# Column order of the input projection in a two-layer hybrid encoder: both gates of HGRN heads 0 and 1 first, the queries second, and the HGRN work beside the third unit

## The chip, the cores and the metric

The kernel runs on one core of one Trainium2 chip. The metric is the device time of one execution in microseconds (us). An execution of the kernel before took 1639.49 us in the median of 3 runs (1636.96 to 1640.6). Engines are named as in the profile: PE (TensorE matmuls), PEld (its weight loads), DVE (VectorE), ACT (ScalarE), POOL (GpSimd), SP (SyncE, which issues the weight loads from memory here).

## What is computed

One sequence of 512 tokens with 1024 features goes through two layers. Each layer has a mixer and then a mixture of 16 experts. The mixer projects the normalised input with one matrix of 4608 columns, and cuts the result into nine groups of 512 columns:

```
proj = xn @ w_in                      # (512, 1024) x (1024, 4608)
rq, rk, rv, rg, hq, hf_fwd, hf_bwd, hi, hg = split(proj, 9)
q = rotary(rq); k = rotary(rk) * 128**-0.5          # 4 retention heads
r_out = rms(retention(q, k, rv)) * ret_g * silu(rg)
q2 = silu(hq) * 128**-0.5;  v2 = hi                 # 4 HGRN heads of 128
f  = lb + (1 - lb) * sigmoid(z);  k = (1 - lb) * sigmoid(-z)   # z = hf_fwd or hf_bwd
h_out = rms(hgrn(q2, k_f, v2, log f_f) + reversed hgrn with f_b, k_b) * hgrn_g * silu(hg)
h = x + concat(r_out, h_out) @ w_out
```

Each HGRN head needs its query, its forward gate and its backward gate; the values v2 are needed only by the last part of its recurrence. The first layer has lb = 0.

## The kernel before, in words

**The projection.** `plan` queues the weight loads in the order of `GROUPS`: column group 4 (hq), 5 (hf_fwd), 6 (hf_bwd), 7 (hi), 0, 1, 2, 3 (the retention groups) and 8 (hg). I call the nine projections unit 0 to unit 8, in the order in which they run. A unit has 96 matmuls of 128x512 and takes four PSUM banks, one for each 128 columns (c = 0 to 3). Its weights come in two loads of 1 MB (512 rows by 512 columns). `split` (L423) cuts them into four parts of 256 rows. ACT rounds a part to the matmul's format (L436, "copy"), and DVE subtracts the rounded part from the part (L438, "low part"); for the odd parts of the units with columns 7 and 2 POOL does the subtraction. Every product is a sum of three matmuls, two with the rounded part and one with the low part. Unit n is cut into quarters q = 0 to 3, one for each part; at the start of quarter q the code issues the split of the next part, 4n+q+1. The four banks are complete one after the other in the last quarter, and each is evacuated there: `silu_q` (one ACT, one DVE instruction), `forget` (two ACT instructions, in the second layer two of DVE as well), `copy_out` (one ACT), `rotate` (two ACT of 64 partitions, one DVE, one POOL, and one DVE addition that `add_late` issues with the next bank).

**The work beside it.** `proj` yields after every six matmuls, 16 times in a unit. I call these steps 1 to 16. After each step `lead` (L812) adds a budget to a credit that begins at 0 in each unit, and while the credit is above 0 it issues the next piece of the work beside the projection and takes off the piece's cost. Nothing here is measured at run time: budgets (`BUDGET`, L420) and costs are constants, and each engine runs its instructions in the order of issue. So the pieces' places are worked out by adding.

**The HGRN pieces** (`hgrn_pair`, heads 0 and 1, then heads 2 and 3), each once per head, with its cost:

- A (1.2): POOL adds the two keys (L568), DVE multiplies gates and queries (L569).
- B (1.2): two DVE products (L579, L580), ACT rounds them (L582), POOL subtracts (L583).
- C (1.3): two DVE products (L551, L556), two ACT copies that make the keys of the next level (L531), one POOL product (L561).
- D (0.65): four PE products with `parity` (L591), one DVE product (L594).
- L1 to L6 (1.9 each, the two heads by turns): four PE products with the keys that the piece of this head before it made (L604), the same two DVE products, two ACT copies and one POOL product as C, and one DVE selection (L606).
- T (0.4): transposes (L619) and ACT copies; S (1.0): products (L644) and DVE sums (L650), the first that read v2; O (0.5): outputs (L663).

In the kernel before the pieces of heads 0 and 1 begin beside unit 3 with budget 1.0 (A, A, B, B, C in steps 1 to 5, C in 7, D in 8 and 9). Those of heads 2 and 3 begin at the last step of unit 4 (budget 1.2) and go on beside unit 5 (budget 1.0: B, B in steps 2 and 3, C, C in 4 and 5, D, D in 7, level pieces in 8, 10, 12, 14, 16) and unit 6 (budget 0.9: level pieces in steps 1, 3, 5 and so on). Unit 7 (budget 2.2) has the rest of them, then `retention`, whose pieces are keys (1.0), outputs (0.6) and states (1.0) by head, and then four splits of the output weights (L806 ACT, L807 two on POOL and two on DVE). The keys of head 0 come in step 1 and its states in step 2. The last outputs and two output splits come in step 6, the other two splits in step 7.

Of the kernel before, what the change touches and what calls it, by code (L numbers as in the profile page):

```python
# [16 lines left out]
P = 128  # L17
S = 512
# [47 lines left out]
class Kernel:  # L66
# [55 lines left out]
    def plan(self):  # L122
        a = self.a
        for l in range(self.depth):
            for g in self.GROUPS:
                for j in range(2):
                    n = 2 if g == self.GROUPS[0] and j == 0 else 1
                    self.wq.append((("in", l, g, j),
                                    [a["w_in"][l, j * 512 + i * (512 // n):j * 512 + (i + 1) * (512 // n),
                                               g * 512:(g + 1) * 512]  # L130
                                     .rearrange("(k p) c -> p k c", p=P) for i in range(n)], [n, 4 // n, 512]))
            for f in range(2):
                for j in range(2):
                    self.wq.append((("out", l, f, j), a["w_out"][l, j * 512:(j + 1) * 512, f * 512:(f + 1) * 512]
                                    .rearrange("(k p) c -> p k c", p=P), [4, 512]))
            for q in range(NE // 2):

                for j in range(2 if q == 0 else 0):
                    for nm in ("w_gate", "w_up"):
                        self.wq.append(((nm, l, -1, j), [a[nm][l, e, :2 * P].rearrange("(p k) c -> k p c", k=2)[j]  # L140
                                                         for e in range(2)], [2, 1024]))
                for j in range(q == 0, 4):
                    for nm in ("w_gate", "w_up"):
                        for e in (2 * q, 2 * q + 1):
                            self.wq.append(((nm, l, e, j), a[nm][l, e, j * 256:(j + 1) * 256, :]
                                            .rearrange("(p k) c -> p (k c)", k=2), [2, 1024]))
                if q < NE // 2 - 1:
                    for j in range(4):
                        for e in (2 * q, 2 * q + 1):
                            self.wq.append((("w_down", l, e, j), a["w_down"][l, e, j * 256:(j + 1) * 256, :]  # L150
                                            .rearrange("(p k) c -> p (k c)", k=2), [2, 1024]))
                else:
                    for i, (lo, n) in enumerate(PIECES):
                        m = 1024 // n
                        for j in range(ND // m):
                            self.wq.append((("w_down", l, i, j),
                                            [a["w_down"][l, e, j * m * P:(j + 1) * m * P, lo:lo + n]
                                             .rearrange("(k p) c -> p k c", p=P) for e in (2 * q, 2 * q + 1)],
                                            [2, m, n]))
# [14 lines left out]
    def load(self, key, src, shape):  # L174
        t = self.slot(shape)
        for i, part in enumerate(src if isinstance(src, list) else [src]):
            dst = t[:, i] if isinstance(src, list) else t

            self.nc.sync.dma_start(dst if len(part.shape) > 2 or isinstance(src, list) else dst.rearrange("p k c -> p (k c)"), part)
        self.loaded[key] = t  # L180
# [236 lines left out]
    WAITS, RATE = (1, 1, 2), 0.7  # L417
    EARLY = 5
    COSTS = (1.2, 1.3, 0.65, 1.9)
    BUDGET = (1.0, 1.2, 1.0, 0.9, 2.2, 1.3)  # L420
    GROUPS = (4, 5, 6, 7, 0, 1, 2, 3, 8)

    def split(self, upto):  # L423


        nc = self.nc
        while self.nsplit <= min(upto, 4 * len(self.GROUPS) - 1):
            i = self.nsplit
            self.nsplit += 1
            g, j, jj = self.GROUPS[i // 4], i % 4 // 2, i % 2  # L430
            if jj == 0:
                self.raw = self.take(("in", self.mix_layer, g, j))
            part = self.slot([2, 2, 512], F32R)
            wh, low = part[:, 0], part[:, 1]
            src = self.raw.rearrange("p a k c -> p (a k) c")[:, 2 * jj:2 * jj + 2]
            nc.scalar.activation(wh, src, AF.Copy)  # L436
            e = nc.gpsimd if self.GROUPS[i // 4] in (7, 2) and i % 2 or i == 0 else nc.vector
            e.tensor_tensor(low, src, wh, op=OP.subtract)  # L438
            self.parts[i] = part
            if jj:  # L440
                self.put(self.raw)
# [31 lines left out]
    def forget(self, l, d, c, ps):  # L473

        nc = self.nc
        F, K = self.F[c // 2][:, c % 2, d], self.K[c // 2][:, c % 2, d]
        nc.scalar.activation(F, ps, AF.Sigmoid)
        nc.scalar.activation(K, ps, AF.Sigmoid, scale=-1.0)
        if l > 0:
            lb, om = self.lb[:, c:c + 1], self.omlb[:, c:c + 1]  # L480
            nc.vector.tensor_scalar(F, F, om, lb, op0=OP.mult, op1=OP.add)
            nc.vector.tensor_scalar(K, K, om, None, op0=OP.mult)
# [51 lines left out]
    def hgrn_pair(self, hp):  # L534
# [6 lines left out]
        Q = self.slot([2, 2, S])  # L541
        AT, T, Tn, kt, B = {}, {}, {}, {}, {}

        def ascend(c, n, m):
# [7 lines left out]
            if 2 * m < P:  # L552
                kt[c] = self.level_keys(B[c][:, n % 2], k0, 2 * m)
            qv = self.view(q0, 0, [[S + m, 2], [2 * m, J], [1, m]])
# [9 lines left out]
        for c in heads:  # L564
            hh = c % 2
            B[c] = self.slot([4, S])
            AT[c], Tn[c] = B[c][:, 2], B[c][:, 3]
            nc.gpsimd.tensor_tensor(AT[c], K[:, hh, 0], K[:, hh, 1], op=OP.add)  # L568
# [4 lines left out]
        for c in heads:  # L573


            q0, k0, x = Q[:, c % 2], K[:, c % 2], B[c][:, :2]
            X[c] = self.slot([2, 2, S], F32R)
# [32 lines left out]
        for c in heads:  # L610
            part = lambda x: x[:, :3 * P].rearrange("p (b t) -> p b t", b=3)
            W[c] = [part(B[c][:, 0]), part(B[c][:, 1]), part(F[:, c % 2, 0]), part(F[:, c % 2, 1])]
        for c in heads:
# [211 lines left out]
    def mixer(self, l):  # L825
        nc = self.nc
        self.norm1(l)
        self.rope = self.tmp4([2, S])
        nc.sync.dma_start(self.rope, self.a["rope"])
        if l == 0:  # L830
            self.const_rows()
        self.lead(self.proj(0, False, self.silu_q))
        if l == 0:
            self.more_consts()
        self.F = [self.slot([2, 2, S]) for _ in range(2)]
        self.K = [self.slot([2, 2, S]) for _ in range(2)]
        for n, d in ((1, 1), (2, 0)):
            self.lead(self.proj(n, False, lambda c, ps: self.forget(l, d, c, ps)))
        self.oh = None
        self.hsq = self.t2.tile([P, S], F32, name=f"hsq{l}", tag="tn", bufs=1)  # L840
        hg = self.hgrn()
        B = self.BUDGET
        self.lead(self.proj(3, True, lambda c, ps: self.copy_out("v2", c, ps)), hg, B[0])
        self.left = ()
        for n, nm in ((4, "rq"), (5, "rk")):
            self.lead(self.proj(n, False, lambda c, ps: self.rotate(nm, c, ps)), hg, B[n - 3])
        self.add_late()
        self.lead(self.proj(6, True, lambda c, ps: self.copy_out("rv", c, ps)), hg, B[3])
        wo = self.wout_split(l)

        def eighth():
            yield from hg
            yield from self.retention()
            for _ in range(4):
                yield next(wo)
        side = eighth()
        self.lead(self.proj(7, False, lambda c, ps: self.gate_out("rg", 4 * l, c, ps)), side, B[4])
        for _ in side:
            pass

        def ninth():
            yield from self.norms()
            yield from wo
        side = ninth()
        self.lead(self.proj(8, False, lambda c, ps: self.mix_out(8 + 4 * l, c, ps)), side, B[5])
        for _ in side:
            pass
        self.put(*self.xH, *self.xL, self.oh)
        self.load_h(self.hd if l > 0 else self.xv)
        self.xe = self.slot([ND, 2 * P])  # L870
        self.pump()
        self.output(l)
# [497 lines left out]
```

## Time and profile before

| | |
|---|---|
| median of 3 runs | 1639.49 us (1636.96 to 1640.6) |
| profiled execution | 1637.67 us, of which the span is 1635.8 us |
| granted TensorE clock, mean | 0.977 of full speed |
| PE busy | 1531.0 us (94%) |
| DVE, ACT, POOL busy | 664.4, 474.9, 229.3 us |
| units 0 to 8, layer 0 | from 15.4 to about 298 us of the span |
| units 0 to 8, layer 1 | from 821.6 to about 1107 us of the span |

The span runs from the first to the last instruction; the profiled execution took 1.87 us more than its span. A line of the timeline has start, duration, engine, source line, operation, tiles, shape and count, and in brackets how long the engine was idle before it and what ended that. Neighbouring instructions of one kind are merged. A stretch's clock is the share of the full TensorE clock that was granted.

### The profile page before, as it was taken

To read this page: it belongs to the slowest core of one execution; us is meant where nothing else is said; L and a number is where in the kernel's file an instruction comes from. 1 tells how busy PE (TensorE), PEld (TensorE's weight loads), DVE (VectorE), ACT (ScalarE), POOL (GpSimd) and SP (SyncE) were. 2 spreads that over 40 slices of the span, in tenths; PEclk is the share of its full clock that TensorE was granted. 3 is DMA by queue.
4 is the path that set the end of the run, shared out by engine and by line. 5 is a ranking of instruction groups with operands and counts; after the bars stand their busy time and mean duration, and the time that the engine had idled before them with its cause. 6 is when DMAs were issued, how large, how long until landed. Compare 5 with 4: busy or idle time off the path is not lost. (4 is left out here: it accounts for less than half of the span.)

```text
span 1635.8 us, 19932 instructions
## 1 busy us (share of the span) xinstructions
PE 1531.0 (94%) x7970; PEld 954.9 (58%) x7970; DVE 664.4 (41%) x1107; ACT 474.9 (29%) x889; POOL 229.3 (14%) x201
## 2 busy tenths in 40 slices
PE   7989899969999999999999899999699999999986
PEld 6878798754354534533478787977444445444333
DVE  5378945561121312212254889464511122212113
ACT  4334444542221200200343434455322202112003
POOL 3042542100000000011021344430000000000201
PEclk9999999989999999999999999999799999999998
DMA  7211132577999999999941211317699999999997
GB/s 262 75 53 52 52 124 78 211 303 301 427 425 426 427 426 427 426 427 427 400 176 51 78 41 64 123 52 258 273 385 427 420 427 426 427 427 426 426 426 275
DMA packets 94605, 464.53 MB, mean 284 GB/s; under 512 B 7904, under 2 KB 16288, under 8 KB 48432
## 3 DMA queue, kind: packets, MB, share of 16 engines
q1 hardware_dynamic: 93040, 458.35, 69.0%
q0 software_dynamic: 1472, 4.90, 0.8%
q8 instruction: 63, 1.03, 0.2%
q14 instruction: 30, 0.25, 0.0%
HBM read 459.03 MB, written 4.19 MB: 283 GB/s over the span
## 5 line engine op out<-in xcount | busy, mean ns | idle before, releaser
L1145 PE MATMUL pj<-s,s 128*64 128x512 f32 x2048 | 478.8, 599 | 19.2 <-DMA s<-in_w_up_dram 13.9
L465 PE MATMUL pj<-s,s 128*128 128x512 f32 x1728 | 426.7, 401 | 12.9 <-DVE s L438 8.6
L465 PEld LDWEIGHTS pj<-s,s 128*128 128x128 f32 x1728 | 324.2, 192 | 82.7 <-DVE s L438 11.6
L1145 PEld LDWEIGHTS pj<-s,s 128*64 128x64 f32 x2048 | 173.3, 137 | 279.6 <-issue 203.3
L1265 PE MATMUL pb<-s,t 128*64 128x512 f32 x896 | 197.8, 594 | 5.4 <-ACT t L1183 2.7
L1272 POOL TENSOR_TENSOR s<-s,s 128x1024 f32<-128x1024 f32 x8 | 18.7, 2362 | 872.1 <-DVE s L1205 823.5
L1265 PEld LDWEIGHTS pb<-s,t 128*64 128x64 f32 x896 | 66.0, 137 | 126.8 <-issue 110.8
L1193 DVE SCALAR_TENSOR_TENSOR t<-pb,sm,t 128x512 fp32r<-128x512 f32 (+1 forms) x34 | 24.5, 719 | 242.5 <-ACT t L1192 241.0
L1205 DVE TENSOR_TENSOR s<-s,pb 128x512 f32<-128x512 f32 (+1 forms) x112 | 67.3, 661 | 130.0 <-PE pb L1200 130.0
L909 PE MATMUL pj<-s,s 128*128 128x512 f32 x384 | 96.6, 400 | 3.4 <-DVE s L796 2.9
L438 DVE TENSOR_TENSOR s<-s,s 128x1024 fp32r<-128x1024 f32 x62 | 84.3, 1383 | 37.8 <-ACT s L436 37.6
L1110 DVE COPY sm<-pb 128x2 f32<-128x2 f32 x16 | 2.5, 159 | 210.9 <-PE pb L1107 210.9
L909 PEld LDWEIGHTS pj<-s,s 128*128 128x128 f32 x384 | 69.3, 189 | 20.7 <-DVE s L796 4.6
L1192 ACT ACTIVATE t<-pb,sm 128x512 fp32r<-128x512 f32 (+1 forms) x34 | 22.5, 662 | 195.4 <-PE pb L1265 183.2
L1088 PEld LDWEIGHTS pb<-t,t 128*128 128x128 f32 x512 | 64.9, 199 | 17.3 <-issue 15.0
L1121 ACT ACTIVATE t<-pb 128x512 fp32r<-128x512 f32 x16 | 9.6, 601 | 221.0 <-PE pb L1119 221.0
L436 ACT ACTIVATE s<-s 128x1024 fp32r<-128x1024 f32 x72 | 73.4, 1048 | 0.0
L1088 PE MATMUL pb<-t,t 128*128 128x256 f32 x512 | 69.8, 293 | 3.2 <-DVE t L1072 2.4
L1200 PE MATMUL pb<-t,t 128*128 128x512 f32 (+1 forms) x256 | 66.7, 401 | 0.1
L556 DVE TENSOR_TENSOR s<-s,s 128x512 f32<-128x512 f32 x56 | 59.3, 1059 | 13.4 <-PE pb L604 13.4
L1200 PEld LDWEIGHTS pb<-t,t 128*128 128x128 f32 x256 | 44.7, 188 | 33.0 <-issue 19.4
L531 ACT ACTIVATE s<-s 128x256 f32<-128x256 f32 x96 | 35.3, 415 | 93.8 <-DVE s L551 93.5
(237 smaller groups left out, 1541.2 us busy)
## 6 DMA issues: line engine op xcount, KB each, us to landing
s<-in_w_gate_dram SPq DMA_DIRECT2D x124, 1024.0 KB, 19.5
s<-in_w_up_dram SPq DMA_DIRECT2D x124, 1024.0 KB, 19.6
s<-in_w_down_dram SPq DMA_DIRECT2D x112, 1024.0 KB, 19.6
s<-in_w_in_dram SPq DMA_DIRECT2D x34, 1024.0 KB, 5.9
s<-in_w_down_dram SPq DMA_DIRECT2D x32, 512.0 KB, 9.4
s<-in_w_out_dram SPq DMA_DIRECT2D x8, 1024.0 KB, 4.8
s<-in_x_dram SPq DMA_DIRECT2D x8, 512.0 KB
s<-in_w_gate_dram SPq DMA_DIRECT2D x8, 512.0 KB, 5.6
```

What stands on the lines that cost most here:

```text
L436: nc.scalar.activation(wh, src, AF.Copy)
L438: e.tensor_tensor(low, src, wh, op=OP.subtract)
L465: nc.tensor.matmul(pg[c], lhsT=lhsT, rhs=rhs, start=(k == 0 and m == 0), stop=(k == ND - 1 and m == 2))
L531: self.nc.scalar.activation(kv[:, :, e], src, AF.Copy)
L556: v.tensor_tensor(qv, qv, tq, op=OP.mult)
L909: nc.tensor.matmul(po, lhsT=x, rhs=w, start=(k == 0 and i == 0), stop=(k == ND - 1 and i == 2))
L1088: nc.tensor.matmul(pt[:, i], lhsT=x[:, tt, k % 2::2], rhs=oh[:, tt], start=(tt == 0 and x is self.picked[u][0]), stop=(tt == NT - 1 and x ...
L1145: nc.tensor.matmul(pg[n + 2 * f][e * CAP:(e + 1) * CAP], lhsT=self.xe[:, k, at + e * CAP:at + (e + 1) * CAP], rhs=w[e][:, f * 512:(f + 1) ...
L1193: v.scalar_tensor_tensor(yL[0][:, cs], py, gate, yH[0][:, cs], op0=OP.mult, op1=OP.subtract)
L1200: nc.tensor.matmul(pc, lhsT=ohT[:, tt * P:(tt + 1) * P], rhs=y[:, cs], start=(y is yH[0]), stop=(y is yL[0]))
L1205: v.tensor_tensor(dst, dst, pc, op=OP.add)
L1265: nc.tensor.matmul(py[f][e * CAP:(e + 1) * CAP], lhsT=hT[:, k, e * CAP:(e + 1) * CAP], rhs=W[e][:, k2, f * 512:(f + 1) * 512], start=(k == ...
```

## The change

`GROUPS` becomes `UNITS`, a list of column starts. Unit 0 now has the first 256 columns of hf_fwd and the first 256 of hf_bwd (both gates of heads 0 and 1). Unit 1 has the queries. Unit 2 has the other halves of the two gates. Units 3 to 8 have the columns that they had. The loads of units 0 and 2 are cut by columns: twice as many DMAs, in rows of 1 KB instead of 2 KB, of 256 KB for the first half of unit 0 and of 512 KB else. The HGRN pieces begin beside unit 2, with new budgets. The POOL subtractions stay with the odd parts of units 3 and 6. No arithmetic is added or left out.

```diff
     def plan(self):
...
-            for g in self.GROUPS:
+            for g, unit in enumerate(self.UNITS):
                 for j in range(2):
-                    n = 2 if g == self.GROUPS[0] and j == 0 else 1
+                    n = 2 if g == j == 0 else 1
+                    m, w = 4 // n, 512 // len(unit)
                     self.wq.append((("in", l, g, j),
-                                    [a["w_in"][l, j * 512 + i * (512 // n):j * 512 + (i + 1) * (512 // n),
-                                               g * 512:(g + 1) * 512]
-                                     .rearrange("(k p) c -> p k c", p=P) for i in range(n)], [n, 4 // n, 512]))
+                                    [((slice(i * m, (i + 1) * m), slice(e * w, (e + 1) * w)),
+                                      a["w_in"][l, j * 512 + i * m * P:j * 512 + (i + 1) * m * P, at:at + w]
+                                      .rearrange("(k p) c -> p k c", p=P)) for i in range(n) for e, at in enumerate(unit)], [4, 512]))
...
-    BUDGET = (1.0, 1.2, 1.0, 0.9, 2.2, 1.3)
-    GROUPS = (4, 5, 6, 7, 0, 1, 2, 3, 8)
+    BUDGET = (0.95, 0.95, 0.9, 0.9, 1.4, 1.3, 0.9)
+    UNITS = ((2560, 3072), (2048,), (2816, 3328), (3584,), (0,), (512,), (1024,), (1536,), (4096,))
...
-            e = nc.gpsimd if self.GROUPS[i // 4] in (7, 2) and i % 2 or i == 0 else nc.vector
+            e = nc.gpsimd if g in (3, 6) and i % 2 or i == 0 else nc.vector
...
     def forget(self, l, d, c, ps):
+        if c // 2 not in self.F:
+            self.F[c // 2], self.K[c // 2] = self.slot([2, 2, S]), self.slot([2, 2, S])
...
-        self.lead(self.proj(0, False, self.silu_q))
+        self.F, self.K = {}, {}
+        self.lead(self.proj(0, False, lambda c, ps: self.forget(l, 1 - c // 2, c % 2, ps)))
         if l == 0:
             self.more_consts()
-        self.F = [self.slot([2, 2, S]) for _ in range(2)]
-        self.K = [self.slot([2, 2, S]) for _ in range(2)]
-        for n, d in ((1, 1), (2, 0)):
-            self.lead(self.proj(n, False, lambda c, ps: self.forget(l, d, c, ps)))
+        self.lead(self.proj(1, False, self.silu_q))
...
         hg = self.hgrn()
         B = self.BUDGET
+        self.lead(self.proj(2, False, lambda c, ps: self.forget(l, 1 - c // 2, 2 + c % 2, ps)), hg, B[-1])
         self.lead(self.proj(3, True, lambda c, ps: self.copy_out("v2", c, ps)), hg, B[0])
```

Unit 2 gets budget 0.9, unit 3 0.95, units 4 to 6 get 0.95, 0.9 and 0.9, unit 7 gets 1.4 and unit 8 keeps 1.3.

## Rows read from the trace of the kernel before

**Rows 1.** Page: busy time of engines; a group's count, busy, mean ns, idle before.

```profile
PE 1531.0 (94%) x7970; PEld 954.9 (58%) x7970; DVE 664.4 (41%) x1107; ACT 474.9 (29%) x889; POOL 229.3 (14%) x201
...
L436 ACT ACTIVATE s<-s 128x1024 fp32r<-128x1024 f32 x72 | 73.4, 1048 | 0.0
```

**Rows 2.** PE's waits, 80 to 275 us (layer 0): us in total, times, longest.

```profile
PE pb L591 <- POOL s L583: 4.5, 3, 2.2
PE pj L465 <- DVE s L438: 3.7, 2, 2.0
PE pb L604 <- ACT s L531: 2.4, 1, 2.4
```

**Rows 3.** Timeline of PE: units 1 to 3 of layer 0, then of layer 1.

```profile
54.73 39.16 PE L465 MATMUL pj<-s,s 128*128 128x512 f32 x172
...
96.55 1.01 PE L591 MATMUL pb<-s,parity 128*128 128x512 f32 x2 [2.19 <-POOL s L583]
...
99.95 2.50 PE L465 MATMUL pj<-s,s 128*128 128x512 f32 x5 [1.96 <-DVE s L438]
...
835.83 65.36 PE L465 MATMUL pj<-s,s 128*128 128x512 f32 x287 [0.99 <-DVE s L438]
...
908.64 2.50 PE L465 MATMUL pj<-s,s 128*128 128x512 f32 x5 [2.19 <-DVE s L438]
```

**Rows 4.** Timelines of DVE and POOL, start of unit 3, layer 0.

```profile
88.81 2.18 DVE L579 TENSOR_TENSOR s<-s,s 128x512 f32<-128x512 f32 x1 [6.65 <-POOL s L568]
...
96.47 3.42 DVE L438 TENSOR_TENSOR s<-s,s 128x1024 fp32r<-128x1024 f32 x1 [2.07 <-ACT s L436]
...
103.91 1.27 DVE L594 TENSOR_TENSOR s<-pb,two 128x512 f32<-128x512 f32 x2
...
93.43 5.38 POOL L583 TENSOR_TENSOR s<-s,s 128x1024 fp32r<-128x1024 f32 x2 [3.40 <-ACT s L582]
```

**Rows 5.** Timeline of PE: end of unit 4 and start of the second pair, layer 0.

```profile
144.77 1.50 PE L644 MATMUL pb<-s,s 128*128 128x128 f32 x12
...
150.22 4.63 PE L663 MATMUL pb<-s,s 128*128 128x128 f32 x40
...
165.63 1.20 PE L591 MATMUL pb<-s,parity 128*128 128x512 f32 x4 [0.75 <-POOL s L583]
168.41 1.17 PE L591 MATMUL pb<-s,parity 128*128 128x512 f32 x2 [1.58 <-POOL s L583]
```

**Rows 6.** Stretches of layer 0: length, busy by engine, granted clock, DMA share, GB/s.

```profile
169.00:173.00 4.00, 4.00 (x17) 3.32 (x16) 4.00 (x3) 0.57 (x2) 3.80 (x3) 0.64 0.55 177
196.00:201.00 5.00, 5.00 (x21) 4.16 (x20) 5.00 (x6) 0.98 (x4) 3.90 (x4) 0.68 0.00 0
```

**Rows 7.** Timelines of DVE, ACT and PE around the end of unit 5, layer 0.

```profile
182.35 1.22 DVE L438 TENSOR_TENSOR s<-s,s 128x1024 fp32r<-128x1024 f32 x1 [0.56 <-ACT s L436]
...
184.18 1.28 DVE L523 TENSOR_TENSOR s<-s,t 128x512 f32<-128x512 f32 x1
...
188.80 0.59 ACT L513 ACTIVATE t<-pj 64x512 f32<-64x512 f32 x1
...
194.40 0.72 ACT L531 ACTIVATE s<-s 128x256 f32<-128x256 f32 x2 [3.19 <-DVE s L551]
...
195.18 1.54 PE L604 MATMUL pb<-s,s 128*128 128x128 f32 x8 [2.42 <-ACT s L531]
```

**Rows 8.** Timelines of PE, ACT and DVE in unit 7 of layer 0.

```profile
231.15 1.64 PE L465 MATMUL pj<-s,s 128*128 128x512 f32 x6
...
267.17 6.87 PE L465 MATMUL pj<-s,s 128*128 128x512 f32 x29 [1.74 <-DVE s L438]
...
231.21 1.05 ACT L723 ACTIVATE s<-pb,dec_k 128x384 f32<-128x384 f32 x2 [0.51 <-PE pb L720]
...
258.00 3.90 ACT L806 ACTIVATE s<-s 128x1024 fp32r<-128x1024 f32 x4
...
260.05 5.93 DVE L807 TENSOR_TENSOR s<-s,s 128x1024 fp32r<-128x1024 f32 x2 [5.93 <-ACT s L806]
```

More of the change, by code (lines that the diff above doesn't have):

```diff
@@ L177, in load @@
             dst = t[:, i] if isinstance(src, list) else t
+            if isinstance(part, tuple):
+                (k, cols), part = part
+                dst = t[:, k, cols]
             self.nc.sync.dma_start(dst if len(part.shape) > 2 or isinstance(src, list) else dst.rearrange("p k c -> p (k c)"), part)
@@ L419 @@
     COSTS = (1.2, 1.3, 0.65, 1.9)
-    BUDGET = (1.0, 1.2, 1.0, 0.9, 2.2, 1.3)
-    GROUPS = (4, 5, 6, 7, 0, 1, 2, 3, 8)
+    BUDGET = (0.95, 0.95, 0.9, 0.9, 1.4, 1.3, 0.9)
+    UNITS = ((2560, 3072), (2048,), (2816, 3328), (3584,), (0,), (512,), (1024,), (1536,), (4096,))
     def split(self, upto):
         nc = self.nc
-        while self.nsplit <= min(upto, 4 * len(self.GROUPS) - 1):
+        while self.nsplit <= min(upto, 4 * len(self.UNITS) - 1):
             i = self.nsplit
             self.nsplit += 1
-            g, j, jj = self.GROUPS[i // 4], i % 4 // 2, i % 2
+            g, j, jj = i // 4, i % 4 // 2, i % 2
             if jj == 0:
@@ L434, in split @@
             wh, low = part[:, 0], part[:, 1]
-            src = self.raw.rearrange("p a k c -> p (a k) c")[:, 2 * jj:2 * jj + 2]
+            src = self.raw[:, 2 * jj:2 * jj + 2]
             nc.scalar.activation(wh, src, AF.Copy)
-            e = nc.gpsimd if self.GROUPS[i // 4] in (7, 2) and i % 2 or i == 0 else nc.vector
+            e = nc.gpsimd if g in (3, 6) and i % 2 or i == 0 else nc.vector
             e.tensor_tensor(low, src, wh, op=OP.subtract)
```

## The prediction

> **What bounds the kernel now.** I read the page first: PE is busy for 94% of the span [rows 1], so the change, which keeps every product, can only touch PE's waits and the clock that PE is granted. Then I read PE's waits by what ended them. In units 1 to 7 of layer 0 they come to 10.6 us [rows 2], and layer 1 repeats the pattern, with a longer part at the start of the first pair. The timeline puts them at four places: the start of the first pair of HGRN heads in unit 3 (2.19 and 1.96 us, [rows 3]), the start of the second pair in unit 5 (0.75 and 1.58, [rows 5]), the rotation at the end of unit 5 (2.42, [rows 7]) and the output splits in unit 7 (1.74, [rows 8]). The stretches come last. After the second and the third place the granted clock averages 0.64 over 4 us and 0.68 over 5 us [rows 6], so PE spent part of these stretches at the lower of its two levels (1.2 instead of 2.4 GHz); against the full clock that is 4 x 0.36 = 1.4 and 5 x 0.32 = 1.6 us lost. After the fourth it isn't so: 29 matmuls took 6.87 us [rows 8], 0.24 us each. If every one of these waits went, with the clock that they cost, the two layers would gain under 30 us. That is the most that the change could do.
>
> A step of six matmuls takes 6 x 39.16/172 = 1.37 us [rows 3], half a unit 10.93. I add the pieces' costs against the new budgets as the code does, and follow each engine's queue from the start of a unit.
>
> **The start of the first pair (now unit 2).** The pieces stand at the same steps as before (A, A, B, B in 1 to 4), so the low part of the third quarter is again issued behind B on DVE and behind its rounding on ACT. Before, unit 3 of layer 0 began 10.93 us before the end of the first row of [rows 3], at 82.96, and PE went on with the third quarter at 99.95, 17.0 us later; in layer 1 it began at 890.26 and went on at 908.64, 18.4 us later. Now POOL has no subtraction in this unit and its key sums run early, since the gates are two units old. The queries come last: bank 3 is evacuated by ACT (0.6, as the 0.59 of [rows 7]), then part 9 is rounded (1.05, [rows 1]) and subtracted (1.22, [rows 7]) until about 2.9; the two A products of the same size end at 5.3; the first B product I put at 1.1, between the half of 1.22 and the 2.18 of the row beside POOL. So it ends at 6.4. From the end of that product to the end of the low part the row has 99.89 - 90.99 = 8.9 us, since the subtraction takes 3.42 us beside POOL's pair of 5.38 us [rows 4]. The low part is there at 15.3 and PE, which wants it at 11.2, waits 4.1 us. It goes on 1.7 us earlier than before in layer 0 and 3.1 in layer 1, less the first D piece, which then fell into the wait and now doesn't (4 products, 0.9 us): **-0.8 and -2.2 us**. The bounds are none and all of the old waits (4.15, and in layer 1 the 1.4 more). The loss of clock that follows I leave as it was.
>
> **The start of the second pair (now unit 4).** T, T and S of the first pair are in step 1 of unit 4, S in 2, O in 3 and 4, A in 5 and 6, B in 7 and 8. S takes 1.3 us and T the same, O half of 4.5 [rows 5], so the first O ends at about 3 x 1.37 + 3 x 1.3 + 2.2 = 10.2. Behind its copy part 18 is rounded and subtracted until 13.1; A, A and one B product last until 16.5, and 8.9 us later, at 25.4, part 19 is ready. PE wants it after 12 steps, 8.4 us of T, S and O and 0.9 of D, at 25.7. So there is no wait, and the 2.33 us and the 1.4 us of clock go: **-3.8 us** in each layer. Bounds: -3.8 and, if the DVE comes 3 us later, 0. The three pieces in step 1 cost 0.2 us, as S waits for T's copies (0 to 0.4).
>
> **The rotation at the end of unit 4.** What is late next is here. Before, only T, S and O lay beside it, and nothing waited. Now C is in steps 10 and 11, D in 12 and 13, the level pieces in 14 and 16 and then in 1 and 3 of unit 5: the same places as those of level pieces at the end of unit 5 before, where the one of step 3 waited 2.42 us. The C pieces are over 103.91 - 90.99 = 12.9 us after the B product [rows 4], at 29.4. Behind them are part 20's rounding, then the rotation. Before, it took 6.45 us from the low part (182.35) to the end of the first key copy (188.80, [rows 7]); without the addition of an older bank (1.28) and with one D product (0.64) it takes 5.8, from 30.6 to 36.4. PE is at the piece of step 1 at 35.2: 1.2 us of wait. From ACT's start on the next bank to the end of the next key copy the rows have 195.12 - 188.80 = 6.3 us, so that is at 42.7, and PE wants it at 40.0: 2.65 us. With the clock of the row (1.6) this is **+5.4 us** in each layer. Bounds: 0, as here before, and +7.
>
> **The rotation at the end of unit 5.** The level pieces are in steps 13 and 15 and in 1 and 3 of unit 6, one step earlier than those that were late. Both keys are in time by the same queue; but ACT, which waits for DVE in its order of issue, gets to bank 3 and to POOL's part 25 later, and PE waits some 0.9 and 1.7 us for them, with a clock as after 0.75 and 1.58 (1.4). The old place cost 2.42 + 1.6. **0**; bounds -4.0 and +2.
>
> **Unit 7.** The keys of head 0 and its states now fall into one step. ACT's two copies between them end 1.05 + 0.06 us after PE is through with the keys [rows 8], which six matmuls covered before: **+1.1 us** (bounds 0 and 1.6). The output splits stand in steps 8 and 9, on both sides of part 31. From the end of the last outputs at 256.75 in the rows, PE would want part 31 after four steps, at 262.4. DVE has the first output split from 260.05 on, 2.96 us beside POOL [rows 8], then part 31 at the same pace with the cover of POOL ending before it does: 265.5. That is 3.1 us in place of 1.74: **+1.4 us**, bounds 0 and +3.7 (1.6 of it clock, if the longer wait costs any).
>
> A rule of the Trainium skill bears on this term: the page SBUF — State Buffer, section SBUF: two separate sides, says that of a DVE operation with two SBUF inputs and a GpSimd operation the one that starts first holds their shared ports for the whole instruction. The low part's 3.42 against 1.22 us agrees. By it part 31 would come either before or wholly behind POOL's second split, not in between.
>
> **At nothing.** The loads of units 0 and 2 move the same bytes in narrower rows; the copies that read the loads had ACT idle for 0.0 us in all before them [rows 1], and in layer 0 PE's first product waits for the norm. ACT's eight evacuations at the end of unit 2 lie beside key copies that PE wants two steps later; if that cover fails, it is a wait like the 1.2 us above, in layer 1 first, where DVE has eight more instructions.
>
> **Sum.** Layer 0: -0.8 - 3.8 + 0.2 + 5.4 + 0 + 1.1 + 1.4 = +3.5; layer 1: +2.1; together +5.6 us. The profiled execution took 1637.67 us, 1.8 less than the median of the runs shown, so the sum gives 1643.3 against it and 1645.1 against the median. I say 1644.
>
> **Rivals.**
> 1. *The rotation of unit 4 hides its keys* (faster). One mechanism: C and D end 4 us sooner on DVE, because POOL's long products miss them. For it: beside unit 4 POOL has no subtraction left. Against it: C's own POOL products follow at once on B's. Then 5.4 us a layer go: 5.6 - 10.8 = -5.2, 1633; if the end of unit 5 is free as well, -13, 1626. It decides at a gain of over 2 us in DVE's queue at C.
> 2. *Gains and losses meet* (no change). Only one of the two waits of unit 4 is there, or the splits of unit 7 cost nothing: 2.8 less or 2.5 less, 1641 with either.
> 3. *DVE gets the ports first in unit 7*: part 31 ends at 260.05 + 2.96 + 1.22 = 264.2, a wait of 1.8, and the term is 0: 1641. The rule of the page in the sentences above is the other way to this result.
> 4. *The gates of unit 2 fill ACT* (slower still). Key copies behind eight evacuations, then POOL's part 13 late: 1.2 us and a clock of 1.6 in each layer, 1650. The copies' lead of two steps speaks against it.
>
> **How the numbers follow.** Forecast 0.39, rivals 0.29, 0.13, 0.07 and 0.12. A difference of 0.2% (3.3 us) can be told from no change. Faster 0.29 is rival 1. Slower is rival 4 and 0.32 of the forecast's 0.39, the rest of which lies under 3.3 us: 0.44. No change: 0.27. The range goes from half-way between rival 1's two times to a little above rival 4: 1629 to 1652; the forecast's own is 1639 to 1650.
>
> **What would show it.** Right: PE's wait for L438 in unit 2 near 4 us; no wait for L583 in unit 4; two waits for L531 in the first three steps of unit 5; a wait for L723 of about 1 us at the start of unit 7; part 31 late by 3 us. Wrong: unit 5 begins without a wait, or unit 2 or 3 has waits that unit 3 did not have before.

## The result: 0.8% slower

Four runs of the changed kernel took 1650.76 to 1653.41 us, median 1651.85; four of the kernel before 1636.96 to 1640.6, median 1638.45. The ratio is 1.0081, with a 95% interval of 1.0064 to 1.0099: 13.4 us slower. The forecast was 1644, between 1629 and 1652, slower with a chance of 0.44. The sign was right, the loss two to three times the +5.6 of the sum. The time lies 0.15 us below the upper end of the range, above the forecast's own 1639 to 1650, and nearest to the 1650 of rival 4, whose waits the trace does not show. The ratios of the experiments below leave out two executions far above the rest, one of the kernel before (1683.45 us, beside numbers 5 to 7) and one of number 8 (8694.58 us), the only one of number 8 with a trace.

**The profile after.** On the page PE is busy for 5.5 us longer than in [rows 1], in a span that is 15.8 us longer; the rest is idle time. Little of the 5.5 us lies in the stretches that the change touches (0.5 us in layer 0, 0.9 in layer 1).

```profile
PE 1536.5 (93%) x7970; PEld 955.4 (58%) x7970; DVE 659.2 (40%) x1107; ACT 476.6 (29%) x889; POOL 227.6 (14%) x201
```

Where does it lie? The first product after unit 8 (L909 before, L916 after) closes the stretch that the change touches. PE's timeline has it in layer 0 and layer 1, first before, then after:

```profile
298.64 1.65 PE L909 MATMUL pj<-s,s 128*128 128x512 f32 x6 [0.26 <-DVE t L790]
...
821.56 3.75 PE L465 MATMUL pj<-s,s 128*128 128x512 f32 x14 [1.51 <-ACT s L398]
...
1107.75 4.15 PE L909 MATMUL pj<-s,s 128*128 128x512 f32 x17 [0.26 <-DVE t L790]
```

```profile
305.78 4.15 PE L916 MATMUL pj<-s,s 128*128 128x512 f32 x17 [0.20 <-DVE t L798]
...
829.69 2.61 PE L471 MATMUL pj<-s,s 128*128 128x512 f32 x9 [1.51 <-ACT s L402]
...
1121.50 2.79 PE L916 MATMUL pj<-s,s 128*128 128x512 f32 x11 [0.18 <-DVE t L798]
```

Layer 0 loses 305.78 - 298.64 = 7.1 us, and layer 1, whose first product was at 821.56 before, (1121.50 - 829.69) - (1107.75 - 821.56) = 5.6: 12.7 of the 13.4. Two layers were predicted to lose 3.5 and 2.1.

PE's waits in layer 0, by what ended them (total, times, longest), answer to [rows 2]. The wait for POOL's subtraction in the B pieces (L583 there, L591 here) is gone from the list, the wait for subtractions (L438 there, L444 here) has nearly doubled, and L612 now waits twice:

```profile
PE pj L471 <- DVE s L444: 6.6, 3, 3.3
PE pb L612 <- DVE s L564: 2.9, 1, 2.9
PE pb L612 <- ACT s L539: 1.7, 1, 1.7
```

The timeline of PE gives each its place. Behind the end of unit 1 they are, mostly in pairs, the start of the first pair in unit 2, the start of the second pair in unit 4 (one row), the rotation at the end of unit 4, that at the end of unit 5, the pieces in unit 6, and unit 7.

```profile
39.30 32.93 PE L471 MATMUL pj<-s,s 128*128 128x512 f32 x144
73.05 0.49 PE L471 MATMUL pj<-s,s 128*128 128x512 f32 x1 [0.81 <-ACT s L442]
76.46 2.50 PE L471 MATMUL pj<-s,s 128*128 128x512 f32 x5 [2.92 <-DVE s L444]
...
150.11 1.42 PE L471 MATMUL pj<-s,s 128*128 128x512 f32 x5 [0.39 <-DVE s L444]
...
161.58 1.16 PE L612 MATMUL pb<-s,s 128*128 128x128 f32 x8 [1.69 <-ACT s L539]
...
168.33 2.04 PE L612 MATMUL pb<-s,s 128*128 128x128 f32 x8 [2.86 <-DVE s L564]
...
201.10 1.89 PE L471 MATMUL pj<-s,s 128*128 128x512 f32 x7 [0.78 <-DVE s L523]
204.50 1.43 PE L471 MATMUL pj<-s,s 128*128 128x512 f32 x5 [1.51 <-POOL s L444]
207.56 0.52 PE L627 MATMUL pb<-ident,s 128*128 128x128 f32 x3 [0.97 <-DVE s L559]
208.80 0.52 PE L627 MATMUL pb<-ident,s 128*128 128x128 f32 x3 [0.72 <-DVE s L614]
...
235.15 1.60 PE L652 MATMUL pb<-s,s 128*128 128x128 f32 x12 [0.97 <-ACT s L731]
...
272.76 8.47 PE L471 MATMUL pj<-s,s 128*128 128x512 f32 x29 [3.29 <-DVE s L444]
```

They add up to 16.9 us against the 10.6 of [rows 2]: 6.3 of layer 0's 7.1. The clock in these stretches (the number before the DMA share) answers to [rows 6]:

```profile
76.00:82.00 6.00, 5.54 (x18) 4.46 (x19) 5.18 (x6) 2.49 (x5) 4.30 (x4) 0.73 0.10 15
150.00:156.00 6.00, 5.89 (x29) 5.02 (x30) 5.35 (x7) 3.09 (x6) 2.40 (x2) 1.00 0.54 178
169.00:174.00 5.00, 5.00 (x24) 4.31 (x24) 4.89 (x7) 1.94 (x6) 0.59 (x2) 0.75 0.10 12
201.00:210.00 9.00, 5.70 (x28) 4.14 (x29) 8.76 (x10) 3.21 (x6) 4.66 (x4) 1.00 0.00 0
273.00:282.00 9.00, 9.00 (x61) 7.13 (x64) 5.37 (x7) 3.74 (x6) 0.00 (x0) 0.81 0.01 2
```

The loss after the second pair and that after unit 5 are gone; two new ones stand after unit 4's rotation (5 x 0.25 = 1.3 us) and after the output splits, where 29 products take 8.47 instead of 6.87 us.

### The profile page after: what moved, and what is told of

It reads as the page before. It is cut to its first block, busy times and chain, and to the rows that moved or that the text cites. A ratio compares the mean times of both kernels' runs of the same rounds, so it can differ in the third digit from the quotient of the medians.

```text
span 1651.6 us, 19953 instructions
## 1 busy us (share of the span) xinstructions
PE 1536.5 (93%) x7970; PEld 955.4 (58%) x7970; DVE 659.2 (40%) x1107; ACT 476.6 (29%) x889; POOL 227.6 (14%) x201
## 4 chain that ended last, share of the span: by engine, by line
PE 61%; DMA 19%; DVE 12%; ACT 5%; issue 3%; POOL 0%; DVEq 0%; SPq 0%; ACTq 0%; POOLq 0%
PE pj L1152 18%; PE pj L471 15%; DMA s<-in_w_up_dram 13%; PE pb L1272 8%; DMA s<-in_w_down_dram 6%; PE pj L916 4%; PE pb L1095 3%; PE pb L612 2%; PE pb L1207 2%; DVE s L444 2%; PE pb L671 2%; PE pb L1238 2%; PE pb L652 1%; ACT s L442 1%; DVE s L531 1%
## 5 line engine op out<-in xcount | busy, mean ns | idle before, releaser
L444 DVE TENSOR_TENSOR s<-s,s 128x1024 fp32r<-128x1024 f32 x62 | 94.0, 1529 | 67.6 <-ACT s L442 67.6
L916 PE MATMUL pj<-s,s 128*128 128x512 f32 x384 | 96.6, 400 | 3.3 <-DVE s L804 2.9
L916 PEld LDWEIGHTS pj<-s,s 128*128 128x128 f32 x384 | 69.3, 189 | 20.6 <-DVE s L804 4.6
L442 ACT ACTIVATE s<-s 128x1024 fp32r<-128x1024 f32 x72 | 74.2, 1048 | 0.1
L539 ACT ACTIVATE s<-s 128x256 f32<-128x256 f32 x96 | 35.2, 415 | 100.5 <-DVE s L559 90.7
L1173 ACT ACTIVATE t<-pj,sm 128x512 f32<-128x512 f32 x32 | 22.0, 687 | 140.4 <-PE pj L1152 140.4
```

The source lines that it names most:

```text
L539: self.nc.scalar.activation(kv[:, :, e], src, AF.Copy)
L916: nc.tensor.matmul(po, lhsT=x, rhs=w, start=(k == 0 and i == 0), stop=(k == ND - 1 and i == 2))
```

## The experiments

**Theory.** What costs time is where the HGRN pieces stand in the engines' in-order queues, beside the two rotations and beside the splits that PE is about to want. **Rival.** The column order itself (more and narrower loads, gates that are older) costs it. Numbers 1 to 4, 5 to 7 and 8 and 9 are three sets, each with the kernel before beside it (1639.36, 1639.3 and 1639.47 us, where the changed kernel had 1638.45), so a difference from the changed kernel is good to about 1 us.

**1. The column order alone.** The HGRN chain goes back beside unit 3, with the budgets of before.

```diff
-    BUDGET = (0.95, 0.95, 0.9, 0.9, 1.4, 1.3, 0.9)
+    BUDGET = (1.0, 1.2, 1.0, 0.9, 2.2, 1.3)
...
-        self.lead(self.proj(2, False, lambda c, ps: self.forget(l, 1 - c // 2, 2 + c % 2, ps)), hg, B[-1])
+        self.lead(self.proj(2, False, lambda c, ps: self.forget(l, 1 - c // 2, 2 + c % 2, ps)))
```

> Column order and loads as changed, but the HGRN pieces begin beside unit 3 again, with the five budgets of the kernel before. Theory (the loss is where the pieces stand against the queues, not the order of the columns): within 2 us of the kernel before, 1637 to 1641. Rival 1 (the narrower loads, or both gates evacuated in units 0 and 2, cost the time): 1646 to 1652.

Measured: 1638.49 us (10 runs) against 1639.36, ratio 0.9995 (0.9986 to 1.0004). Its waits in layer 0 are those of [rows 2] to 0.2 us (4.4 us for POOL's L591, 3.9 for DVE's L444, 2.4 for ACT's L539), and L916 comes as before:

```profile
298.59 4.19 PE L916 MATMUL pj<-s,s 128*128 128x512 f32 x17 [0.27 <-DVE t L798]
```

The order of columns and its narrower rows together cost nothing that can be told (at most 0.7 us by the interval); the whole loss comes with the earlier start and its budgets. The rival falls.

**2. Unit 7 at a lower budget**, so that the output splits come later than part 31.

```diff
-    BUDGET = (0.95, 0.95, 0.9, 0.9, 1.4, 1.3, 0.9)
+    BUDGET = (0.95, 0.95, 0.9, 0.9, 1.0, 1.3, 0.9)
```

> The changed kernel with the budget of unit 7 at 1.0 in place of 1.4: keys and states of head 0 in different steps, all output splits behind the split of part 31. Theory: the wait of 0.97 us for ACT L731 and the one of 3.29 us with 1.6 us of slow clock behind it go in each layer, a wait of up to 1 us for part 32 may come: 8 to 12 us less than the changed kernel, 1640 to 1644. Rival (this time comes back at the start of unit 8, since the output splits and the norms follow later): 1648 to 1652.

Measured: 1647.49 us, ratio to before 1.0049 (1.0034 to 1.0064): 4.4 less than the changed kernel, half of what was expected, and in neither range. Its waits for L731 and for part 31 went, but a part came back in PE's waits of the same unit and the next:

```profile
PE pj L471 <- DVE s L512: 1.5, 1, 1.5
...
PE pb L710 <- ACT t L700: 0.7, 1, 0.7
```

An output split (L815) and the split behind it now lie ahead of the evacuation of a bank (L512) in DVE's queue, and the last output splits spill into unit 8. Here a budget for the whole unit moved the pieces past one urgent thing onto the next.

**3. No rotation.** Its product by the cosines, its product on POOL and the addition are dropped.

```diff
-        sw = self.tmp2()
-        nc.scalar.activation(sw[0:64], ps[64:128], AF.Copy)
-        nc.scalar.activation(sw[64:128], ps[0:64], AF.Copy)
-        nc.vector.tensor_tensor(dst, ps, self.rope[:, 0], op=OP.mult)
-        nc.gpsimd.tensor_tensor(sw, sw, self.rope[:, 1], op=OP.mult)
-        self.add_late(dst, sw)
+        nc.scalar.activation(dst[0:64], ps[64:128], AF.Copy)
+        nc.scalar.activation(dst[64:128], ps[0:64], AF.Copy)
```

> The changed kernel without the rotation's arithmetic: ACT's two copies of 64 partitions write the query or key, and DVE's product, POOL's product and DVE's addition are left out (the output then lacks the rotation). Theory (key copies and bank 3 are late because DVE and ACT stand behind the rotation in their own queues): the waits of 1.69, 2.86, 0.78, 1.51, 0.97 and 0.72 us and 1.6 us of slow clock go in each layer, 16 to 20 us less than the changed kernel, 1632 to 1636. Rival (DVE is late from the C and D pieces alone): the waits of 1.69 and 2.86 stay at half or more, 1642 to 1648.

Measured: 1631.37 us, ratio 0.9944 (0.9927 to 0.9961), 20.5 less than the changed kernel, a little over what was expected. All waits between 156 and 210 us are gone, those of unit 6's pieces among them, so the rival is out; of the list above these stay, with their old sizes:

```profile
PE pj L471 <- DVE s L444: 6.6, 3, 3.3
...
PE pb L648 <- ACT s L727: 1.0, 1, 1.0
PE pj L471 <- ACT s L442: 0.8, 1, 0.8
```

In the changed kernel the waits beside and behind the rotations are 1.69 + 2.86 + 0.78 + 1.51 + 0.97 + 0.72 = 8.5 us, with 1.3 of clock 9.8 us a layer, 19.6 in two. So these waits make nearly the whole of the 20.5 us. That is more than the 13.4 lost, because the kernel before had some 8 us of the same kind (2.42 of wait and 1.6 of clock in each layer).

**4. Every split one step earlier**, from unit 2 on.

```diff
-            self.split(4 * n + q + 1)
+            self.split(4 * n + q + (2 if n > 1 else 1))
```

> The changed kernel with each part's rounding and subtraction issued one quarter of a unit earlier, from unit 2 on. Theory (a low part is late because it is issued behind the pieces): the waits for low parts (0.81 and 2.92 in unit 2, 0.39 in unit 4, 1.51 in unit 6, 3.29 with 1.6 of clock in unit 7) go, but the pieces come 1.2 us later on DVE, and PE then waits some 2 us for the D pieces of unit 2: 10 to 16 us less than the changed kernel, 1636 to 1642. Rival (DVE has no time left there, the waits only move to the pieces): 1648 to 1654.

Measured: 1650.95 us, ratio 1.007 (1.0055 to 1.0085): 0.9 less, nothing that can be told from the changed kernel, as the rival had it. The waits for L444 are gone from PE's list, and the pieces wait instead, L627 alone for 3.7 us:

```profile
PE pb L627 <- DVE s L559: 3.7, 2, 2.8
PE pb L612 <- DVE s L564: 3.2, 2, 2.0
PE pb L612 <- ACT s L539: 2.5, 1, 2.5
```

I read this so: DVE has the same work in front of PE's next products, and sending a split first mostly changes which product finds its input late. What the waits did save, the clock took: in layer 0 they add up to 15.4 in place of 16.9 us, but PE's busy time from unit 1 to unit 8 is 252.3 in place of 249.5 us, with a granted clock of 0.72 from 81 to 87 and 0.57 from 207 to 213 us, behind two of the new waits.

**5. Pauses.** The budget becomes a list by steps: no pieces are drawn in the last four steps of units 4 and 5 and in the first two of units 5 and 6, and more in the other steps of units 5 and 6. All numbers that follow have this loop over steps too; their diffs show the rest.

```diff
-    BUDGET = (0.95, 0.95, 0.9, 0.9, 1.4, 1.3, 0.9)
+    BUDGET = (0.95, [0.95] * 12 + [0] * 4, [0] * 2 + [1.2] * 10 + [0] * 4, [0] * 2 + [1.2] * 14, 1.4, 1.3, 0.9)
...
-        for _ in gen:
+        for step, _ in enumerate(gen):
...
-            credit += budget
+            credit += budget[step] if isinstance(budget, list) else budget
```

> The changed kernel with the whole rotation, but no HGRN piece is issued in the last four steps of units 4 and 5 and in the first two of units 5 and 6; the other steps of units 5 and 6 get budget 1.2, so that all HGRN pieces still end in unit 6. Theory (the loss at the rotations is pieces that stand in one queue with the rotation): most of the waits of 1.69, 2.86, 0.78, 1.51, 0.97 and 0.72 us and the clock behind them go, 14 to 18 us less than the changed kernel, 1633 to 1639. Rival (the rotation alone fills ACT, DVE and POOL, or the denser pieces in the other steps wait instead): 1644 to 1652.

Measured: 1637.09 us (10 runs), ratio 0.9985 (0.9975 to 0.9995), 14.8 less than the changed kernel, with all arithmetic in place. Between 150 and 215 us PE's timeline has one wait above 0.4 us, which is the rotation's own, for its product out of a bank:

```profile
158.01 4.70 PE L471 MATMUL pj<-s,s 128*128 128x512 f32 x18 [1.75 <-DVE s L523]
```

This undoes the loss without undoing the change: the pieces begin as early as in the changed kernel, only none is drawn beside the rotation. It is more than the 13.4 us lost, as the older wait behind unit 5's rotation went too. What is left is mainly the start of unit 2 (0.81 and 2.9 us) and unit 7 (0.97 for L731 and 3.3 for the splits).

**6 and 7. Pauses with and without the earlier split.** Both have pauses in unit 2 too and a slow start of unit 7; number 6 has number 4's earlier split as well. From here on the lines of the code behind `BUDGET` have numbers one higher.

```diff
-    BUDGET = (0.95, 0.95, 0.9, 0.9, 1.4, 1.3, 0.9)
+    BUDGET = (1.05, [1.15] * 12 + [0] * 4, [0] * 2 + [1.25] * 10 + [0] * 4, [0] * 2 + [1.25] * 14,
+              [1.0, 1.1] + [1.8] * 14, 1.3, [1.2] * 4 + [0] * 4 + [1.2] * 8)
...
-            self.split(4 * n + q + 1)
+            self.split(4 * n + q + (2 if n > 1 else 1))
```

> The pauses, and besides: each part is split one quarter earlier from unit 2 on; in unit 2 four steps without a piece between B and C; unit 7 with keys and states of head 0 in two steps and the output splits in steps 7 and 8. Theory (each wait is a place in a queue and can be taken out by pacing): no wait over 1 us is left between unit 2 and unit 7, 12 to 17 us less than before per the two layers' waits of 10.6 and 12 with their clock, 1618 to 1628. Rival (the DVE work has no room, each wait comes back elsewhere): 1635 to 1645.

> The same without the earlier split. Theory (the split's place behind the B pieces and before the output splits makes 2.9 us in unit 2 and 1.7 to 3.3 in unit 7): 6 to 12 us more than with the earlier split, 1627 to 1637. Rival (the pace alone makes the gain): within 2 us of the kernel with the earlier split.

Measured: 1626.75 us with the earlier split, ratio 0.9924 (0.9907 to 0.9941): faster than the kernel before by 12.5 us and than the changed one by 25. Without it 1636.65 (10 runs), ratio 0.9986 (0.9977 to 0.9995), so that the pauses in unit 2 and the slow start of unit 7 by themselves gave nothing that can be told over number 5 (1637.09). The split that gave 0.9 us in number 4 gives 9.9 here, within the 6 to 12 expected: with the pauses an early split takes less from others than it gives. In layer 0 the waits for subtractions, 6.0 us in number 7, are gone in number 6, as are 1.4 us for DVE's L805 at the first products after unit 8; L613, L600 and L711 wait some 5 us more. First number 7's, then number 6's list of PE's waits:

```profile
PE pj L472 <- DVE s L445: 6.0, 2, 3.1
```

```profile
PE pb L613 <- ACT s L540: 2.4, 1, 2.4
PE pj L472 <- DVE s L524: 1.8, 1, 1.8
PE pb L600 <- POOL s L592: 1.8, 2, 1.5
PE pb L711 <- ACT t L701: 1.5, 1, 1.5
```

That no wait above 1 us would be left was wrong: four are, three of them between units 2 and 7 and one (L711) in unit 8.

**8. Three of those four waits taken one by one** (L613, L600, L711), by other pauses and by splits that run no further ahead in unit 8, with the time of number 6 expected to fall.

```diff
-    BUDGET = (0.95, 0.95, 0.9, 0.9, 1.4, 1.3, 0.9)
+    BUDGET = (1.05, [1.15] * 9 + [0] * 7, [0] * 2 + [1.3] * 10 + [0] * 4, [0] * 2 + [1.3] * 14,
+              [1.0, 1.1] + [1.8] * 14, 1.3, [1.2] * 4 + [0] * 2 + [1.25] * 2 + [0] * 2 + [1.1] * 6)
...
-            self.split(4 * n + q + 1)
+            self.split(min(4 * n + q + 2, 32) if 1 < n < 8 else 4 * n + q + 1)
```

> The paced kernel with the earlier split, with three corrections read from its trace: in unit 2 C comes in steps 7 and 8 and the first level piece stays in 12 (its wait of 2.37 us was for a key copy), the D pieces of the second pair come behind the rotation, in step 3 of unit 5 (their wait was 1.53 us), and unit 8 splits no earlier than before (its wait for ACT L701 was 1.52 us). Theory (each wait is a place in a queue): 3 to 5 us a layer less than the paced kernel, 1617 to 1622. Rival (the waits move on to the next piece): 1625 to 1629.

Measured: 1628.09 us, ratio 0.9929 (0.9915 to 0.9942): no better than number 6, whose interval overlaps. The rival was right in its number. Where the waits went stays open, as no trace shows them. One candidate is not shown: the wait of 1.4 us for L805 after unit 8 is in number 7 and, with 1.5 us, in number 9, neither of which splits ahead in unit 8, and number 8 doesn't either.

**9. The same means from unit 3.** The splits of number 8 and pauses, with the chain beside unit 3 again.

```diff
-    BUDGET = (0.95, 0.95, 0.9, 0.9, 1.4, 1.3, 0.9)
+    BUDGET = ([1.2] * 4 + [0] * 2 + [1.2] * 2 + [0] + [1.2] * 7, [1.2] * 12 + [0] * 4, [0] * 2 + [1.25] * 10 + [0] * 4,
+              [0] * 2 + [1.3] * 14, [2.2] * 3 + [1.6] + [1.5] * 12, 1.3)
...
-        self.lead(self.proj(2, False, lambda c, ps: self.forget(l, 1 - c // 2, 2 + c % 2, ps)), hg, B[-1])
+        self.lead(self.proj(2, False, lambda c, ps: self.forget(l, 1 - c // 2, 2 + c % 2, ps)))
```

> The same earlier split and pauses, but the HGRN pieces begin beside unit 3, as in the kernel before, and some of them go into unit 7. If the early start gives room that pacing needs: slower than the paced kernel that starts beside unit 2, 1629 to 1637. Rival (pacing does it all, the early start nothing): 1620 to 1627.

Measured: 1627.66 us, ratio 0.9925 (0.9912 to 0.9937): the rival's side, 0.7 us above its range. With pauses and early splits the start beside unit 3 is as good as the start beside unit 2. The best version, number 6, owes its gain to pacing and splits, not to the early start. The largest waits that remain in number 9's layer 0 are again for DVE, 2.9 us in two and 2.8 in one:

```profile
PE pj L472 <- DVE s L524: 2.9, 2, 1.6
PE pj L472 <- DVE s L513: 2.8, 1, 2.8
```

## Why the prediction came out right in sign and too small

By its own steps, in layer 0, each as the change of its waits and of the clock that follows them:

| step | predicted, us | measured, us |
|---|---|---|
| start of the first pair | -0.8 | -0.4 of wait, -0.2 of clock |
| second pair, with its three pieces in one step | -3.6 | -1.9 and -1.4 |
| rotation, end of unit 4 | +5.4 | +4.6 and +1.3 |
| rotation, end of unit 5, with unit 6's pieces | 0 | +1.6 and -1.6 |
| retention's keys and states | +1.1 | +1.0 |
| output splits | +1.4 | +1.6 and +1.6 |
| sum | +3.5 | +6.0 (+6.3 and, of clock, -0.3; the rows are rounded) |

Layer 0's own difference is 7.1; about 1 us of it stands in no place of the table. So half of layer 0's miss of 3.6 us is one term, the output splits.

**The first pair.** Right. Unit 2 begins 10.93 us before the end of the first row of the timeline, at 61.30, and PE goes on at 76.46, 15.2 us later; 15.3 was worked out. The wait there is 0.81 + 2.92 = 3.7, against 4.1. The 0.81 us, for the rounded part (L442), is a wait that unit 3 didn't have before, which the prediction had listed as a sign of being wrong; it is the first part of the same lateness, one product ahead of the rest. The clock behind it is much as it was, 0.73 over six us here and 0.70 over six before:

```profile
100.00:106.00 6.00, 6.00 (x23) 4.96 (x24) 6.00 (x8) 2.71 (x6) 2.94 (x3) 0.70 0.12 25
```

The 6 x 0.30 = 1.8 us of clock in this row were left out of the prediction's bound of 30 us; with them it is about 32. Nothing else rests on that bound.

**The second pair.** Right, as the wait is 0.39 us; the sum had none.

**Unit 4's rotation.** Right, and it is the heart of the loss: 1.69 and 2.86 us where 1.2 and 2.65 were worked out, at the places named. (The second was to end with a key copy; it ends with DVE's L564 at 168.18, the copy having ended at 168.13.) The queues show how. First DVE, then ACT, around the end of unit 4:

```profile
157.85 0.69 DVE L523 TENSOR_TENSOR s<-pj,t 128x512 f32<-128x512 f32 x1
158.46 1.29 DVE L531 TENSOR_TENSOR s<-s,t 128x512 f32<-128x512 f32 x1
159.67 1.10 DVE L559 TENSOR_TENSOR s<-s,s 128x512 f32<-128x512 f32 x1
160.69 0.68 DVE L564 TENSOR_TENSOR s<-s,s 128x512 f32<-128x512 f32 x1
...
162.78 0.69 DVE L523 TENSOR_TENSOR s<-pj,t 128x512 f32<-128x512 f32 x1 [0.77 <-ACT t L522]
```

```profile
160.80 0.72 ACT L539 ACTIVATE s<-s 128x256 f32<-128x256 f32 x2 [2.99 <-DVE s L559]
161.55 0.59 ACT L521 ACTIVATE t<-pj 64x512 f32<-64x512 f32 x1
```

ACT stands idle for 2.99 us in front of the key copy of a piece (L539), which waits for DVE's L559, and that waits behind the rotation on DVE (L523, L531). ACT's copies of the next bank (L521), which the rotation needs, come only after it. So each engine holds what the other's next instruction needs. Numbers 3 and 5 remove one half of this pair each, and in both the two waits are gone.

**Unit 5's rotation.** Right in the sum by luck, as two errors cancel. The two waits are 0.78 and 1.51 (0.9 and 1.7 predicted). The clock that the forecast still had there didn't fall (1.00 from 201 to 210), but the pieces of unit 6 wait 0.97 + 0.72 us more, which no step had. In number 3, without the rotation, these are gone too.

**Keys and states.** Right, with 0.97 against 1.1.

**The output splits: the step of which the size was wrong.** The wait is 3.29 us (3.1 predicted, 1.74 before). But the clock that it costs had been priced at nothing, because after 1.74 us it had not fallen [rows 8], and 1.6 us were only in the bound. It fell: 29 products took 8.47 us. That is the largest of the misses, 1.8 us a layer. DVE and POOL in unit 7 show the wait itself:

```profile
266.83 2.59 DVE L815 TENSOR_TENSOR s<-s,s 128x1024 fp32r<-128x1024 f32 x1 [6.10 <-ACT s L814]
269.34 3.37 DVE L444 TENSOR_TENSOR s<-s,s 128x1024 fp32r<-128x1024 f32 x1
272.63 1.21 DVE L815 TENSOR_TENSOR s<-s,s 128x1024 fp32r<-128x1024 f32 x1
```

```profile
265.92 2.42 POOL L815 TENSOR_TENSOR s<-s,s 128x1024 fp32r<-128x1024 f32 x1 [4.03 <-ACT s L814]
268.82 2.80 POOL L815 TENSOR_TENSOR s<-s,s 128x1024 fp32r<-128x1024 f32 x1 [0.48 <-ACT s L814]
```

DVE's two subtractions end 1.08 and 1.09 us after the ends of POOL's two, and one with no POOL beside it takes 1.21: so their work lies behind POOL's, not beside it. The Trainium skill says so (SBUF — State Buffer, section SBUF: two separate sides: of a DVE instruction with two SBUF inputs and a GpSimd instruction that reads SBUF, whichever starts first has the shared ports for the whole instruction), and this trace agrees: part 31 came wholly behind POOL's second split.

**The rivals.** The first, that the rotation hides its keys, is out by the waits at 161.58 and 168.33. The second is out as both waits of unit 4's rotation and that of unit 7 are there. The third, that DVE gets the ports first, by the rows above. The fourth, that unit 2's gates fill ACT, is out as no wait stands at the end of unit 2; that its 1650 is the number nearest to the measured time is chance.

**What isn't told.** Layer 1's measured 5.6 is 3.5 over its term, by the same places (its waits in unit 7 are 0.97 and 3.28 us). Outside of the two stretches the profiled execution is 3.1 us longer than before, but it was the longest of its four, 1.6 above their median, and the one before 0.8 below the median of its own; whether any of the rest is the change's isn't settled.

## To carry to other kernels

Side work that was drawn into in-order queues at an even rate cost most here where the main work has its own chain over the same engines: try to draw none of it during that chain, and more outside of it (14.8 us here). An earlier issue of what was late gave nothing that can be told by itself (0.9 us) and much together with such pauses (9.9 us), so try the two together before either is dropped. And after a wait that grows, price the clock that the next products are granted as well.

## What the hardware did that was not expected

The clock did not follow the length of the waits alone. It fell after single waits of 2.86, 2.92 and 3.29 us (0.75, 0.73 and 0.81 in the stretches above, so that PE was for part of each at the lower of its levels, 1.2 instead of 2.4 GHz), but four waits of 4.0 us in all between 201 and 210, with PE at work between them, left it at 1.00, while 0.75 and 1.58 us [rows 5] had lowered it to 0.64 [rows 6]. PE's busy time in layer 0 from unit 1 on is therefore almost the same in both kernels, 249.0 us before and 249.5 after:

```profile
39.00:299.00 260.00, 248.99 (x1359) 211.78 (x1359) 170.71 (x214) 112.74 (x197) 90.59 (x83) 0.97 0.20 70
```

```profile
39.00:305.80 266.80, 249.48 (x1358) 211.25 (x1358) 171.37 (x217) 112.05 (x194) 88.67 (x79) 0.98 0.20 68
```
